# Hybrid Hyena and GLA block: attention operands stored in the layout in which they are loaded, projection columns regrouped, and the sums of the second product's weights set later

## The chip, the cores and the metric

One core of one Trainium2 chip runs the whole block in one launch. The metric is the device time of one launch in microseconds (us). The kernel before has three runs, and one more execution was profiled.

The core's engines each work through an instruction queue of their own: TensorE (PE, matrix products, with its weight loads listed as PEld), VectorE (DVE), ScalarE (ACT), GpSimd (POOL) and SyncE (SP, which here issues nearly all DMA transfers). Semaphores tie them together. An instruction whose input isn't there yet stops everything behind it in its own engine's queue.

## The reference

One layer of a diffusion backbone, in float32, on 2048 tokens of width 1024, with 256 context tokens ahead of them:

```python
h_lat = _rms_norm(x, norm_mix) * (1 + sc1) + sh1
hy, q, k, v, og, gf, gb = split(h_lat @ w_in)        # 1536, 256, 256, 512, 512, 16, 16 columns
# context tokens: the same projection gives only the start states s_f, s_b of the attention
y_gla = (rms(gla_forward + gla_backward) * g_norm) * silu(og)      # 4 heads, chunks of 64 tokens
y_hy  = x0 * (long_conv(x1 * v))                     # FFT convolution over 2048 tokens, 512 channels
x = x + g1 * (concat(y_hy, y_gla) @ w_out)
h2 = _rms_norm(x, norm_mlp) * (1 + sc2) + sh2
x = x + g2 * (square(relu(h2 @ w_mlp1)) @ w_mlp2)    # 1024 -> 4096 -> 1024
out = _rms_norm(x, norm_final)
```

The filter's spectrum for the long convolution is computed in the kernel too.

## The kernel before, in words

Every float32 operand of a product is split into a rounded high part and a low rest, and one product becomes three matmuls (high by high, high by low, low by high). The two MLP products also use a seven-product scheme for 2 by 2 blocks (Strassen's kind), so the blocks of both matrices are added and subtracted before they are multiplied.

The work runs in stages. All times here are microseconds of the profiled execution.

- To about 270: the filter network, its spectrum (`kernel_steps`, `second` stores pieces of it to the DRAM tensor `d_s`), and the context path (`context_steps`).
- 270 to 830: the projections of the 2048 tokens. `token_major(grp, w, tbs)` multiplies blocks of 128 tokens by 264 columns of `w_in`. The 1056 columns of v, og and the two gates make four groups (`grp` 0 to 3) of 264 columns, so a group may hold the end of v and the start of og, or the end of og and the 32 gate columns. v goes by DVE to the DRAM tensor `d_v`, og by Silu on ACT and a multiplication on POOL to `d_og`, and the gates are kept for a transpose.
- 830 to about 1125: the convolution (`conv_steps`, 32 turns: two halves of the channels with 16 turns each), interleaved with the attention (`states`, `weights`, `outputs`). A convolution turn `t` loads four DFT blocks every second turn (tiles `dff`, `dfi`) and the spectrum's real and imaginary pieces (`kr`, `ki`). PE multiplies by `dff` (L945), ACT copies to `sw`, DVE multiplies `kr` (L951, L953), POOL multiplies `sw` by `ki` (L952), and PE goes on with `kr` (L962). The pools hold 2 `dff`, 3 `dfi`, 5 `kr` and 3 `ki`. Attention loads a whole head of v (`vv`, 1 MB), of keys (`kt`, 1 MB) and og in quarters (`og`).
- to about 1960: the output product, then the first MLP product (`ps`, L1384), whose results go through DRAM (`d_m`).
- 1960 to 2679: the second MLP product, 64 turns named `at`, which are 8 passes over 8 blocks of 256 tokens. A turn has 7 products of 6 matmuls each (`full2`, L1640). After each, DVE adds the result into `acc` (`more`, L1645) and the PSUM buffer becomes free for PE. ACT rounds the next turn's left operand (`uh`, L1597), POOL makes its rest (`ul`, L1598).

Every four turns of the second product a new 1 MB piece of `w_mlp2` is loaded to a tile `raw`. Its four quarters are multiplied by the gate `g2` on POOL (`gate`, L1461), and then DVE makes two differences of them, the sums of the change's name:

```python
lambda: dve.tensor_sub(r[:, 4, :], r[:, 3, :], r[:, 0, :]),   # L1464
lambda: dve.tensor_sub(r[:, 3, :], r[:, 2, :], r[:, 3, :])    # L1465
```

`split` (L231, L232) then makes high and low parts of them. `slot()` is called six times in a turn and takes one such step off the list `prep` each time. The code's order is only a wish. The instructions of each engine are arranged when the program is built, by data, buffers and estimated durations, so a step can stand well ahead of the place at which the code calls it.

At the start of the second product `load_u(0)`, `load_u(1)`, `load_acc(0)`, `load_u(2)` and `load_acc(1)` are called in this order. `load_u` fills a tile `ur` with two or three transfers, `load_acc` fetches 1 MB of residual rows.

Of the kernel before, what the change touches and what calls it, by code (L numbers as in the profile page):

```python
# [10 lines left out]
F32 = mybir.dt.float32  # L11
# [7 lines left out]
P = 128  # L19
D = 1024  # L20
T = 2048
# [103 lines left out]
def layout(x):  # L125
# [36 lines left out]
    o["wada1"] = np.stack([blk(wa[:, i * 256:(i + 1) * 256]) for i in range(8)])  # L162
    o["wada2"] = np.stack([blk(wa[:, 2 * D + i * P:2 * D + (i + 1) * P]) for i in range(32)])
    wi = x["w_in"][0]
    o["wi_vg"] = np.stack([blk(wi[:, 2048 + i * 264:2048 + (i + 1) * 264]) for i in range(4)])
    two = lambda a, b: np.concatenate([blk(wi[:, a:a + P]), blk(wi[:, b:b + P])], axis=2)
    o["wi_qk"] = np.stack([two(1536 + i * P, 1792 + i * P) for i in range(2)])
    o["wi_xv"] = np.stack([two(512 + i * P, 1024 + i * P) for i in range(4)])
    o["wi_x0"] = np.stack([blk(wi[:, i * P:(i + 1) * P]) for i in range(4)])
# [41 lines left out]
def hybrid_block(ctx: ExitStack, tc, a, out, dbg=None):  # L211
# [20 lines left out]
        dve.tensor_sub(lo, src, hi.bitcast(F32))  # L232

    dr = ctx.enter_context(tc.tile_pool(name="dram", bufs=1, space=DRAM))
    d_s = dr.tile([32, 128, DH], F32, name="d_s")
    d_s0 = dr.tile([1, DH], F32, name="d_s0")
    d_q = dr.tile([2, 256, T], F32, name="d_q")
    d_ki = dr.tile([2, 256, T], F32, name="d_ki")
    d_kt = dr.tile([NH, P, 16, 2, 64], F32, name="d_kt")
    d_dec = dr.tile([2, 256, 32], F32, name="d_dec")  # L240
    d_v = dr.tile([T, 512], F32, name="d_v")
    d_og = dr.tile([T, 512], F32, name="d_og")
    d_u = dr.tile([DH, T], F32, name="d_u")
    d_x0 = dr.tile([DH, T], F32, name="d_x0")
    d_yt = dr.tile([D, T], F32, name="d_yt")
# [108 lines left out]
    with ExitStack() as ek:  # L354
# [114 lines left out]
        def context_steps():  # L469
# [11 lines left out]
            yield from norm_out(xc, hch, hcl, 1)  # L481
            vc = xp.tile([P, 2, 512], F32, name="vc")
            gc = xp.tile([P, 2, 32], F32, name="gc")
            for g_, c0, n in ((3, 232, 32), (0, 0, 264), (1, 0, 264)):
                hi, lo = load_w(a["wi_vg"][g_][:, :, c0:c0 + n])
                for i in range(2):
                    pp = pt("pc")
                    for k in range(KD):
                        ts = slice(i * P, (i + 1) * P)
                        mm3(pp[:, 0:n], hch[:, k, ts], hcl[:, k, ts], hi[:, k, 0:n], lo[:, k, 0:n],  # L490
                            k == 0, k == KD - 1)
                    if g_ == 0:
                        nc.scalar.copy(vc[:, i, 0:264], pp[:, 0:264])
                    elif g_ == 1:
                        nc.scalar.copy(vc[:, i, 264:512], pp[:, 0:248])
                    else:
                        nc.scalar.copy(gc[:, i, :], pp[:, 0:32])
                    yield W["c_proj"]
# [57 lines left out]
        def kernel_steps():  # L556
            for hc in range(2):
# [73 lines left out]
                def second(t):  # L631
                    zt, dff = st.pop(t)
                    kk = 2 * t
                    pu = pt("pu")
                    for s in range(2):
                        q = (kk + s) % 4
                        mm(pu[:, s * 256:(s + 1) * 256], dff[:, q * P:(q + 1) * P], zt[:, s * 256:(s + 1) * 256],
                           start=True, stop=True)
                    ks = kt_("kb", "ks")
                    nc.scalar.copy(ks[:], pu[:])  # L640
                    k3 = ks[:].rearrange("p (k c) -> p k c", k=2)
                    if t == 0:

                        dma(d_s0[:, cs], k3[127:128, 0, :])
                        dma(d_s[0, 127:128, cs], zrow[0:1, :])
                        dma(d_s[0, 0:127, cs], k3[0:127, 0, :])
                        dma(d_s[1, :, cs], k3[:, 1, :])
                    else:
                        dma(d_s[kk:kk + 2, :, cs].rearrange("k p c -> p k c"), k3)

                yield from staged(16, fetch, turn, second, w=W["k_turn"])

# [16 lines left out]
    rst = ap.tile([P, 512], F32, name="rst")  # L669
    dma(rst[:], a["reset"])  # L670

    def token_major(grp, w, tbs):

        c0 = 264 * grp
        hi, lo = w
        vn = max(0, min(264, 512 - c0))
        on = min(1024 - c0, 264) - vn
        o0 = max(0, c0 - 512)
        for tb in tbs:
            if grp == 3:  # L680
                gs = ap.tile([P, 4, 32], F32, tag="gs", bufs=2, name="gs")
            for i in range(4):
                pp = pt("pv")
                ts = slice(i * P, (i + 1) * P)
                for k in range(KD):
                    mm3(pp[:, 0:264], hts[tb][0][:, k, ts], hts[tb][1][:, k, ts], hi[:, k, :], lo[:, k, :],
                        k == 0, k == KD - 1)
                rows = slice(tb * 512 + i * P, tb * 512 + (i + 1) * P)
                st = ap.tile([P, 512], F32, tag=("gt1", "glg")[i % 2], bufs=2, name="st")
                if vn:  # L690
                    dve.tensor_copy(st[:, 0:vn], pp[:, 0:vn])
                    dma(d_v[rows, c0:c0 + vn], st[:, 0:vn])
                if on:
                    act(st[:, vn:vn + on], pp[:, vn:vn + on], AF.Silu)
                    gps.tensor_mul(st[:, vn:vn + on], st[:, vn:vn + on], gnf[:, o0:o0 + on])
                    dma(d_og[rows, o0:o0 + on], st[:, vn:vn + on])
                if grp == 3:
                    dve.tensor_copy(gs[:, i, :], pp[:, 232:264])
                yield 2.7
            if grp == 3:  # L700
                pg = pt("pg")
                for i in range(4):
                    tr(pg[0:32, i * P:(i + 1) * P], gs[:, i, :], ident)
                dve.tensor_copy(gt[tb * 32:(tb + 1) * 32, :], pg[0:32, :])

    def mod_block(j):
# [116 lines left out]
    def load_kv(h, part=None):  # L823
        if part != 1:
            kt = pre.tile([P, 16, 2, 64], F32, tag="kt", bufs=1, name="kt")
            dma(kt[:], d_kt[h])
            heads[h, "kt"] = kt
        if part != 0:
            vv = gpool(h).tile([P, 16, P], F32, tag="vv", bufs=1, name="vv")
            dma(vv[:], d_v[:, h * P:(h + 1) * P].rearrange("(b p) e -> p b e", p=P))  # L830
            heads[h, "kv"] = (heads[h, "kt"], vv)

    def load_u(ct):
# [48 lines left out]
    def conv_steps():  # L882
        for hc in range(2):
# [29 lines left out]
            def k0(t):  # L913
                kk = 2 * t
                if t % 2 == 0:
                    st["f", t // 2] = ft("dff", 2, "dff")
                    dma(st["f", t // 2][:], a["dft_f"][:, kk:kk + 4, :].rearrange("p k n -> p (k n)"))
                    st["i", t // 2] = ft("dfi", 3, "dfi")
                    dma(st["i", t // 2][:], a["dft_i"][:, kk:kk + 4, :].rearrange("p k n -> p (k n)"))
                kr, ki = ft("kr", 5, "kr"), ft("ki", 3, "ki")  # L920
                for h in range(2):
                    hs = slice(h * 64, (h + 1) * 64)
                    dma(kr[hs].rearrange("p (k c) -> p k c", k=2), d_s[kk:kk + 2, 0:64, cs].rearrange("k p c -> p k c"))
                    dma(ki[hs].rearrange("p (k c) -> p k c", k=2), d_s[kk:kk + 2, 64:128, cs].rearrange("k p c -> p k c"))
                if t == 0:
                    dma(kr[127:128, 0:256], d_s0[:, cs])
                st["k", t] = (kr, ki)
# [181 lines left out]

    def load_og(h, q):  # L1110
        og = gp.tile([P, 4, P], F32, tag="og", bufs=4, name="og")
        dma(og[:], d_og[q * DH:(q + 1) * DH, h * P:(h + 1) * P].rearrange("(b p) e -> p b e", p=P))
        heads[h, "og", q] = og

    def outputs(h, q):
# [274 lines left out]
    def keep(ps, tag):  # L1390
        t = us.tile([P, 512], F32, tag=tag, bufs=2, name=tag)
        nc.scalar.copy(t[:], ps[:])  # L1392
        return t
# [58 lines left out]

    w2s, w2r = {}, {}

    def w2_raw(n, engs):

        r = w2r[n] = raw_tile()
        dma(r[:, 0:4, :], a["w2"][n])

        def gate(q):  # L1460
            engs[q].tensor_mul(r[:, q, :], r[:, q, :], g2b[:, (q // 2) * 512:(q // 2 + 1) * 512])  # L1461

        return [*(lambda q=q: gate(q) for q in range(4)),
                lambda: dve.tensor_sub(r[:, 4, :], r[:, 3, :], r[:, 0, :]),  # L1464
                lambda: dve.tensor_sub(r[:, 3, :], r[:, 2, :], r[:, 3, :])]  # L1465

    def w2_split(n, m):
        r, j, k = w2r[n], PR[m][1], PR[m][0]
# [11 lines left out]
    for tb in range(2):  # L1480
# [8 lines left out]
        for at in range(1, 16):  # L1489
# [33 lines left out]
            if at == 15 and tb == 0:  # L1523
                raws.append(fill_raw(1, 1, gps))
            elif at == 15:
                more_w2 = w2_raw(1, [dve, gps, gps, dve])
                for q in (1, 2):
                    more_w2.pop(1)()
            full(x, w, 6, False)
            u2 = keep(x, "u2")  # L1530
            first(6)
# [5 lines left out]
                nxt[5] = w_split(rn, 5)  # L1537
            full(x, w, 7, False)
            u3 = keep(x, "u3")
            put(n, tb, 1, 1, y, u3)  # L1540
            first(7)
            if rn is not None:
# [56 lines left out]
        ops[at, m] = (hi, lo)  # L1599

    load_u(0)
    load_u(1)
    first_u.update({(h, m): u_tile(0, h, m) for h, m in U0})
    acc4 = {}

# [8 lines left out]
        return acc4[t // 2][:, 2 * (t % 2) + i, j * 512:(j + 1) * 512]  # L1614

    load_acc(0)
    for m in (1, 2, 6):
        w2_split(1, m)
        split_u(0, m)
# [1 line left out]
        w2_split(1, m)  # L1621
    load_u(2)
    load_acc(1)
    held = []
    for f in puts:
        f()
    for step in held:
# [44 lines left out]
    def slot():  # L1672

        for todo in (prep, ends):
            if todo:
                todo.pop(0)()

    sums, prep, ends = {}, [], []
    late = None
# [1 line left out]
    for at in range(NU):  # L1681
# [25 lines left out]
            load_acc(t + 2)  # L1707
        if at + 3 < NU:
            load_u(at + 3)
        if at % 4 == 0:  # L1710
            coming = w2_raw(row(at + 4, 1, 1 - at // 4 % 2), [gps] * 4)
        if at == 40:
            nf = mf.tile([P, D], F32, name="nf")
            dma(nf[:], a["norm_final"].partition_broadcast(P))
# [55 lines left out]
```

## Time and profile before

| | |
|---|---|
| runs | 2690.41, 2690.08, 2682.15 us; median 2690.08 |
| profiled execution | 2681.11 us, span 2679.3 us, mean granted clock 0.963 |
| mean memory traffic | 152 GB/s; 406.09 MB in 304480 packets |
| packets under 2 KB | 226712 |
| HBM read, written | 273.49 MB, 130.09 MB |

The span runs from the first to the last instruction. The granted clock is the share of full speed that TensorE was given. Busy time of an engine is a sum over stages with different limits, so the stages are read one by one. An idle stretch of PE is put down to what released it.

### The profile page before, as it was taken

The page shows a single profiled execution, that of the slowest core. Times are in us where ns is not written, and L with a number is a line of the kernel's source. Part 1 is how long each engine was busy: PE and PEld are TensorE (multiplying, and loading weights), DVE is VectorE, ACT ScalarE, POOL GpSimd, SP SyncE. Part 2 cuts the span into 40 slices and gives each one's busy share as a digit, 9 for nine tenths or more (in the row PEclk, how much of TensorE's full clock was granted, in tenths as well). Part 3 has the DMA queues.
Part 4 walks back from the last instruction along what each step waited for, and adds up shares of the span by engine and source line. Part 5 has one row for each costly group of instructions (what it writes and reads, how often), then busy time and mean ns, then how long its engine had stood idle before and what let it go on. Part 6 is the DMA issues. An engine that isn't in the chain of part 4 may idle for free. (4 is left out here: it accounts for less than half of the span.)

```text
span 2679.3 us, 38019 instructions
## 1 busy us (share of the span) xinstructions
PE 2497.2 (93%) x13320; PEld 2068.7 (77%) x13320; DVE 1613.7 (60%) x2619; ACT 1186.3 (44%) x2273; POOL 1077.1 (40%) x1093
## 2 busy tenths in 40 slices
PE   9799999999998788899989998999978999998997
PEld 5678978898887777788778887888857777777776
DVE  5754366735567677744465557555565656565668
ACT  6464352225225555434555555555543333333334
POOL 2130231214112223132244443544456666666575
PEclk9899999999998798899999999999989999999999
DMA  5425444432547777556444545545474233323233
GB/s 195 147 80 175 124 135 141 139 110 98 175 148 198 202 242 199 198 164 212 154 149 138 165 139 169 170 140 165 135 285 151 99 114 105 119 101 114 99 132 135
DMA packets 304480, 406.09 MB, mean 152 GB/s; under 512 B 25108, under 2 KB 226712, under 8 KB 293920
## 3 DMA queue, kind: packets, MB, share of 16 engines
q1 hardware_dynamic: 301408, 395.27, 46.7%
q10 hardware_dynamic: 2880, 8.39, 0.8%
q8 instruction: 105, 1.72, 0.3%
q14 instruction: 87, 0.71, 0.1%
HBM read 273.49 MB, written 130.09 MB: 151 GB/s over the span
## 5 line engine op out<-in xcount | busy, mean ns | idle before, releaser
L1598 POOL TENSOR_TENSOR ul<-ur,uh 128x256 fp32r<-128x256 f32 x441 | 362.5, 830 | 209.6 <-ACT uh L1597 208.3
L1645 DVE TENSOR_TENSOR acc<-acc,ps 128x512 f32<-128x512 f32 x448 | 303.8, 682 | 153.4 <-PE ps L1640 150.4
L1597 ACT CAST uh<-ur 128x256 fp32r<-128x256 f32 x448 | 179.8, 406 | 408.8 <-PE ps L1640 387.5
L1384 PE MATMUL ps<-bh,wh 128*128 128x512 f32 x896 | 350.4, 393 | 5.8 <-ACT u L1392 3.1
L1384 PE MATMUL ps<-bl,wh 128*128 128x512 f32 x896 | 351.0, 392 | 4.1 <-DVE bl L232 4.1
L1384 PE MATMUL ps<-bh,wl 128*128 128x512 f32 x896 | 350.4, 392 | 4.1 <-DVE wl L232 4.1
L232 DVE TENSOR_TENSOR wl<-raw,wh 128x512 fp32r<-128x512 f32 x276 | 266.7, 978 | 97.0 <-ACT wh L231 94.2
L231 ACT CAST wh<-raw 128x512 fp32r<-128x512 f32 x276 | 170.6, 622 | 201.8 <-PE ps L1384 165.5
L1640 PE MATMUL ps<-wh,uh 128*128 128x512 f32 x448 | 183.5, 410 | 66.4 <-DVE acc L1645 58.2
L1384 PEld LDWEIGHTS ps<-bh,wh 128*128 128x128 f32 x896 | 169.6, 189 | 43.0 <-ACT u L1392 3.7
L1384 PEld LDWEIGHTS ps<-bh,wl 128*128 128x128 f32 x896 | 169.3, 189 | 40.7 <-DVE wl L232 5.3
L1384 PEld LDWEIGHTS ps<-bl,wh 128*128 128x128 f32 x896 | 169.3, 189 | 40.2 <-DVE bl L232 5.3
L1640 PE MATMUL ps<-wh,ul 128*128 128x512 f32 x448 | 179.4, 400 | 0.3 <-DVE ul L1598 0.2
L1640 PE MATMUL ps<-bh,uh 128*128 128x512 f32 x448 | 179.5, 401 | 0.0
L1640 PE MATMUL ps<-bl,uh 128*128 128x512 f32 x448 | 179.5, 401 | 0.0
L1640 PE MATMUL ps<-wl,uh 128*128 128x512 f32 x448 | 179.2, 400 | 0.0
L1640 PE MATMUL ps<-bh,ul 128*128 128x512 f32 x448 | 179.0, 400 | 0.0
L1640 PEld LDWEIGHTS ps<-wh,uh 128*128 128x128 f32 x448 | 87.8, 196 | 96.0 <-DVE acc L1645 63.3
L226 PE MATMUL ph<-hth,whi 128*128 128x512 f32 x384 | 150.9, 393 | 0.0
L226 PE MATMUL pv<-whi,hth 128*128 128x264 f32 x512 | 147.2, 288 | 2.8 <-ACT whi L231 2.6
L228 PE MATMUL ph<-hth,wlo 128*128 128x512 f32 x384 | 149.6, 390 | 0.2 <-DVE wlo L232 0.2
L227 PE MATMUL ph<-htl,whi 128*128 128x512 f32 x384 | 149.4, 389 | 0.0
(289 smaller groups left out, 5713.1 us busy)
## 6 DMA issues: line engine op xcount, KB each, us to landing
raw<-in_w_dram SPq DMA_DIRECT2D x49, 1024.0 KB, 5.5
ur<-d_m SPq DMA_DIRECT2D x112, 448.0 KB, 3.7
d_m<-c SPq DMA_DIRECT2D x128, 256.0 KB, 2.5
d_m<-s SPq DMA_DIRECT2D x96, 256.0 KB, 3.4
xt<-in_x_dram SPq DMA_DIRECT2D x32, 512.0 KB, 5.0
mwt<-in_wada_dram SPq DMA_DIRECT2D x64, 256.0 KB, 3.0
raw<-in_wi_vg_dram SPq DMA_DIRECT2D x20, 528.0 KB, 4.8
wada<-in_wada_dram SPq DMA_DIRECT2D x16, 512.0 KB, 7.6
```

The source lines that it names most:

```text
L226: mm(ps, lh, rh, start=first, stop=False)
L227: mm(ps, lh, rl, start=False, stop=False)
L228: mm(ps, ll, rh, start=False, stop=last)
L231: nc.scalar.copy(hi, src)
L232: dve.tensor_sub(lo, src, hi.bitcast(F32))
L1384: mm(ps[:], x_[:, sl], y_[j], start=start and i == 0, stop=stop and i == 2, skip_group_check=True)
L1597: nc.scalar.copy(hi[:], src)
L1598: (gps if at else dve).tensor_sub(lo[:], src, hi[:].bitcast(F32))
L1640: mm(ps[:], x_[:, kb, :], y_[:], start=start and kb + i == 0, stop=kb == 1 and i == 2, skip_group_check=True)
L1645: dve.tensor_add(acc(t, i, j), acc(t, i, j), ps[:])
```

## The change

Layout, for the attention and the convolution (the mixers):

- The gate columns are dealt out: each of the four groups now has 256 columns of v or og and 8 gate columns, so groups 0 and 1 are v, groups 2 and 3 are og. `token_major` has one store in place of one or two for a block, and every group copies its 8 gate columns to one tile `gs`. The context path loads the 32 gate columns from an array of their own and takes 256 columns of v at a time.
- `d_v` and `d_og` are laid out by head, then by partition. A load of `vv` reads 8 KB in one piece for a partition and one of `og` 2 KB, where both read pieces of 512 bytes before. The stores write two pieces of 512 bytes for a partition in place of one of 1056, 992 or 928 bytes.
- `d_s` holds, for each half of the channels and each turn, 2 KB in one piece for a partition. `kr` and `ki` are loaded with one transfer of 256 KB each, which reads 64 rows twice (a broadcast), in place of two transfers of 128 KB with pieces of 1 KB.

Second product: in the first piece of weights the two sums go to POOL, for the later pieces the code puts empty slots between the gates and ahead of the sums and calls the load one turn earlier, the piece prepared at the end of the first product has all four gates on DVE, and `load_acc(0)` is called ahead of `load_u(1)`.

```diff
-    d_s = dr.tile([32, 128, DH], F32, name="d_s")
+    d_s = dr.tile([2, 16, 128, 2, 256], F32, name="d_s")
-    d_v = dr.tile([T, 512], F32, name="d_v")
-    d_og = dr.tile([T, 512], F32, name="d_og")
+    d_v = dr.tile([NH, P, 16, P], F32, name="d_v")
+    d_og = dr.tile([NH, P, 16, P], F32, name="d_og")
...
-                        dma(d_s[kk:kk + 2, :, cs].rearrange("k p c -> p k c"), k3)
+                        dma(d_s[hc, t], k3)
...
-                if vn:
-                    dve.tensor_copy(st[:, 0:vn], pp[:, 0:vn])
-                    dma(d_v[rows, c0:c0 + vn], st[:, 0:vn])
-                if on:
-                    act(st[:, vn:vn + on], pp[:, vn:vn + on], AF.Silu)
-                    gps.tensor_mul(st[:, vn:vn + on], st[:, vn:vn + on], gnf[:, o0:o0 + on])
-                    dma(d_og[rows, o0:o0 + on], st[:, vn:vn + on])
-                if grp == 3:
-                    dve.tensor_copy(gs[:, i, :], pp[:, 232:264])
+                if grp < 2:
+                    dve.tensor_copy(st[:, 0:256], pp[:, 0:256])
+                else:
+                    act(st[:, 0:256], pp[:, 0:256], AF.Silu)
+                    gps.tensor_mul(st[:, 0:256], st[:, 0:256], gnf[:, (grp - 2) * 256:(grp - 1) * 256])
+                hs = slice(2 * (grp % 2), 2 * (grp % 2) + 2)
+                dma((d_v, d_og)[grp // 2][hs, :, 4 * tb + i, :].rearrange("h p e -> p h e"),
+                    st[:, 0:256].rearrange("p (h e) -> p h e", h=2))
+                dve.tensor_copy(gs[:, tb, i, 8 * grp:8 * grp + 8], pp[:, 256:264])
...
-            dma(vv[:], d_v[:, h * P:(h + 1) * P].rearrange("(b p) e -> p b e", p=P))
+            dma(vv[:], d_v[h])
...
-                for h in range(2):
-                    hs = slice(h * 64, (h + 1) * 64)
-                    dma(kr[hs].rearrange("p (k c) -> p k c", k=2), d_s[kk:kk + 2, 0:64, cs].rearrange("k p c -> p k c"))
-                    dma(ki[hs].rearrange("p (k c) -> p k c", k=2), d_s[kk:kk + 2, 64:128, cs].rearrange("k p c -> p k c"))
+                for v, hs in ((kr, slice(0, 64)), (ki, slice(64, 128))):
+                    dma(v[:], d_s[hc, t, hs].rearrange("p k c -> p (k c)").partition_broadcast(2))
...
-        dma(og[:], d_og[q * DH:(q + 1) * DH, h * P:(h + 1) * P].rearrange("(b p) e -> p b e", p=P))
+        dma(og[:], d_og[h, :, 4 * q:4 * q + 4, :])
...
-                more_w2 = w2_raw(1, [dve, gps, gps, dve])
-                for q in (1, 2):
-                    more_w2.pop(1)()
+                more_w2 = w2_raw(1, [dve] * 4)
...
     load_u(0)
-    load_u(1)
...
     load_acc(0)
+    load_u(1)
...
-        if at % 4 == 0:
-            coming = w2_raw(row(at + 4, 1, 1 - at // 4 % 2), [gps] * 4)
+        if at == 0:
+            coming = w2_raw(row(4, 1, 1), [gps] * 4, gps)
+        elif at % 4 == 3 and at < 60:
+
+            q = w2_raw(row(at + 5, 1, at // 4 % 2), [gps] * 4)
+            coming = [v for step in q[:4] for v in (None, step)] + [None] * 3 + [q[4], None, q[5]]
```

What the program's order becomes is seen at three places. The first is DVE in the second product (turn 13), where the sums of a new piece stand between the additions into `acc`. Before (L1645 are the additions, L1464 and L1465 the sums, L232 the low parts):

```order
L1645 TENSOR_TENSOR acc<-acc,ps 128x512 x7
L1464 TENSOR_TENSOR raw<-raw 128x512
L1645 TENSOR_TENSOR acc<-acc,ps 128x512
L1465 TENSOR_TENSOR raw<-raw 128x512
L1645 TENSOR_TENSOR acc<-acc,ps 128x512
L232 TENSOR_TENSOR wl<-raw,wh 128x512
```

And now (L1638 are the additions, L1457 and L1458 the sums, L234 the low parts):

```order
L1638 TENSOR_TENSOR acc<-acc,ps 128x512 x7
L1457 TENSOR_TENSOR raw<-raw 128x512
L1638 TENSOR_TENSOR acc<-acc,ps 128x512
L1458 TENSOR_TENSOR raw<-raw 128x512
L1638 TENSOR_TENSOR acc<-acc,ps 128x512
L234 TENSOR_TENSOR wl<-raw,wh 128x512
```

Nothing moved here but the line numbers; from turn 5 to the end all five engines have the same order as before.

The second place is POOL at the start of the second product. Before (L1598 is `ul`, L1461 the gates):

```order
L1598 TENSOR_TENSOR ul<-ur,uh 128x256 x12
L1461 TENSOR_TENSOR raw<-raw,g2b 128x512 x4
L1598 TENSOR_TENSOR ul<-ur,uh 128x256 x21
L1461 TENSOR_TENSOR raw<-raw,g2b 128x512 x3
L1598 TENSOR_TENSOR ul<-ur,uh 128x256
```

And now (L1592 is `ul`, L1454 the gates, L1457 and L1458 the sums):

```order
L1592 TENSOR_TENSOR ul<-ur,uh 128x256 x9
L1454 TENSOR_TENSOR raw<-raw,g2b 128x512 x4
L1592 TENSOR_TENSOR ul<-ur,uh 128x256
L1457 TENSOR_TENSOR raw<-raw 128x512
L1592 TENSOR_TENSOR ul<-ur,uh 128x256
L1458 TENSOR_TENSOR raw<-raw 128x512
L1592 TENSOR_TENSOR ul<-ur,uh 128x256 x15
L1454 TENSOR_TENSOR raw<-raw,g2b 128x512 x3
```

The first piece's gates stand three `ul` earlier and its sums are on POOL. The second piece's gates follow after 17 `ul` in place of 21.

The third place is SP in the convolution's first turns, up to the third load of `dff`, the one at 854.03 in the profile. Before:

```order
L1112 DMA og<-d_og 128x4x128 x2
L826 DMA kt<-d_kt 128x2048
L830 DMA vv<-d_v 128x16x128
L924 DMA ki<-d_s 64x2x256 x2
L917 DMA dff<-in_dft_f_dram 128x512
```

And now:

```order
L1105 DMA og<-d_og 128x512 x2
L825 DMA vv<-d_v 128x2048
L821 DMA kt<-d_kt 128x2048
L1105 DMA og<-d_og 128x512
L1048 DMA dc<-d_dec 64x32
L1049 DMA qi<-d_q 64x2048
L917 DMA ki<-d_s 128x1x512
L912 DMA dff<-in_dft_f_dram 128x512
```

A third `og` quarter (256 KB), a small `dc` and half of a head's queries `qi` (512 KB) came ahead of this `dff`. At the start of the second product SP has the first `acc` load behind two `ur` loads, where it was ahead of all six.

More of the change, by code (lines that the diff above doesn't have):

```diff
@@ L164, in layout @@
     wi = x["w_in"][0]
-    o["wi_vg"] = np.stack([blk(wi[:, 2048 + i * 264:2048 + (i + 1) * 264]) for i in range(4)])
-    two = lambda a, b: np.concatenate([blk(wi[:, a:a + P]), blk(wi[:, b:b + P])], axis=2)
+    two = lambda a, b, n=P, m=P: np.concatenate([blk(wi[:, a:a + n]), blk(wi[:, b:b + m])], axis=2)
+    o["wi_vg"] = np.stack([two(2048 + i * 256, 3072 + i * 8, 256, 8) for i in range(4)])
+    o["wi_gk"] = blk(wi[:, 3072:3104])
     o["wi_qk"] = np.stack([two(1536 + i * P, 1792 + i * P) for i in range(2)])
@@ L483, in context_steps @@
             gc = xp.tile([P, 2, 32], F32, name="gc")
-            for g_, c0, n in ((3, 232, 32), (0, 0, 264), (1, 0, 264)):
-                hi, lo = load_w(a["wi_vg"][g_][:, :, c0:c0 + n])
+            for g_, n in ((2, 32), (0, 256), (1, 256)):
+                hi, lo = load_w(a["wi_gk"] if g_ == 2 else a["wi_vg"][g_][:, :, 0:n])
                 for i in range(2):
@@ L491, in context_steps @@
                             k == 0, k == KD - 1)
[L492 to L495, printed above, removed]
+                    if g_ < 2:
+                        nc.scalar.copy(vc[:, i, g_ * 256:(g_ + 1) * 256], pp[:, 0:256])
                     else:
@@ L644, in second @@
                         dma(d_s0[:, cs], k3[127:128, 0, :])
-                        dma(d_s[0, 127:128, cs], zrow[0:1, :])
-                        dma(d_s[0, 0:127, cs], k3[0:127, 0, :])
-                        dma(d_s[1, :, cs], k3[:, 1, :])
+                        dma(d_s[hc, 0, 127:128, 0], zrow[0:1, :])
+                        dma(d_s[hc, 0, 0:127, 0], k3[0:127, 0, :])
+                        dma(d_s[hc, 0, :, 1], k3[:, 1, :])
                     else:
-                        dma(d_s[kk:kk + 2, :, cs].rearrange("k p c -> p k c"), k3)
+                        dma(d_s[hc, t], k3)
                 yield from staged(16, fetch, turn, second, w=W["k_turn"])
@@ L670, in hybrid_block @@
     dma(rst[:], a["reset"])
+    gs = ap.tile([P, 4, 4, 32], F32, name="gs")
     def token_major(grp, w, tbs):
-        c0 = 264 * grp
         hi, lo = w
-        vn = max(0, min(264, 512 - c0))
-        on = min(1024 - c0, 264) - vn
-        o0 = max(0, c0 - 512)
         for tb in tbs:
-            if grp == 3:
-                gs = ap.tile([P, 4, 32], F32, tag="gs", bufs=2, name="gs")
             for i in range(4):
@@ L687, in token_major @@
                         k == 0, k == KD - 1)
-                rows = slice(tb * 512 + i * P, tb * 512 + (i + 1) * P)
                 st = ap.tile([P, 512], F32, tag=("gt1", "glg")[i % 2], bufs=2, name="st")
-                if vn:
-                    dve.tensor_copy(st[:, 0:vn], pp[:, 0:vn])
-                    dma(d_v[rows, c0:c0 + vn], st[:, 0:vn])
-                if on:
-                    act(st[:, vn:vn + on], pp[:, vn:vn + on], AF.Silu)
-                    gps.tensor_mul(st[:, vn:vn + on], st[:, vn:vn + on], gnf[:, o0:o0 + on])
-                    dma(d_og[rows, o0:o0 + on], st[:, vn:vn + on])
-                if grp == 3:
-                    dve.tensor_copy(gs[:, i, :], pp[:, 232:264])
+                if grp < 2:
[7 more added lines that the diff above has]
+                dve.tensor_copy(gs[:, tb, i, 8 * grp:8 * grp + 8], pp[:, 256:264])
                 yield 2.7
@@ L702, in token_major @@
                 for i in range(4):
-                    tr(pg[0:32, i * P:(i + 1) * P], gs[:, i, :], ident)
+                    tr(pg[0:32, i * P:(i + 1) * P], gs[:, tb, i, :], ident)
                 dve.tensor_copy(gt[tb * 32:(tb + 1) * 32, :], pg[0:32, :])
@@ L1453, in hybrid_block, with w2_raw @@
     w2s, w2r = {}, {}
-    def w2_raw(n, engs):
+    def w2_raw(n, engs, eng=dve):
         r = w2r[n] = raw_tile()
@@ L1463, in w2_raw @@
         return [*(lambda q=q: gate(q) for q in range(4)),
-                lambda: dve.tensor_sub(r[:, 4, :], r[:, 3, :], r[:, 0, :]),
-                lambda: dve.tensor_sub(r[:, 3, :], r[:, 2, :], r[:, 3, :])]
+                lambda: eng.tensor_sub(r[:, 4, :], r[:, 3, :], r[:, 0, :]),
+                lambda: eng.tensor_sub(r[:, 3, :], r[:, 2, :], r[:, 3, :])]
     def w2_split(n, m):
@@ L1539, in hybrid_block @@
             u3 = keep(x, "u3")
+            if tb and at == 15:
+                held = []
             put(n, tb, 1, 1, y, u3)
@@ L1623, in hybrid_block @@
     load_acc(1)
-    held = []
     for f in puts:
@@ L1674, in slot @@
         for todo in (prep, ends):
-            if todo:
-                todo.pop(0)()
+            step = todo.pop(0) if todo else None
+            if step:
+                step()
     sums, prep, ends = {}, [], []
```

## The prediction

> **What bounds the kernel now.** I read the page first: busy time by engine, the DMA queues, and of the groups ACT's casts (busy us, mean ns), and of the DMA issues the row of `ur` (count, KB each, us to landing).
>
> ```profile
> span 2679.3 us, 38019 instructions
> PE 2497.2 (93%) x13320; PEld 2068.7 (77%) x13320; DVE 1613.7 (60%) x2619; ACT 1186.3 (44%) x2273; POOL 1077.1 (40%) x1093
> q1 hardware_dynamic: 301408, 395.27, 46.7%
> q10 hardware_dynamic: 2880, 8.39, 0.8%
> L231 ACT CAST wh<-raw 128x512 fp32r<-128x512 f32 x276 | 170.6, 622 | 201.8 <-PE ps L1384 165.5
> ur<-d_m SPq DMA_DIRECT2D x112, 448.0 KB, 3.7
> ```
>
> PE is the bound, 93% busy. A change that takes no matmul away can win only its 182 us of idle time and the time it runs at a lower clock. So the next view is the busy time by stage: the stretch, then PE, PEld, DVE, ACT and POOL busy, the granted clock, the DMA engines' share and GB/s.
>
> ```profile
> 270.00:830.00 560.00, 554.27 (x3095) 476.44 (x3094) 315.19 (x594) 186.98 (x316) 130.49 (x138) 0.99 0.43 135
> 830.00:860.00 30.00, 21.25 (x180) 17.56 (x179) 26.94 (x60) 16.67 (x30) 4.62 (x4) 0.88 0.94 236
> 860.00:900.00 40.00, 32.01 (x290) 28.48 (x292) 26.47 (x52) 22.11 (x42) 16.12 (x16) 0.80 0.74 200
> 900.00:930.00 30.00, 22.87 (x145) 20.74 (x144) 21.00 (x50) 15.79 (x30) 4.57 (x4) 0.73 0.89 262
> 930.00:990.00 60.00, 54.91 (x591) 48.42 (x590) 42.71 (x97) 29.31 (x52) 8.25 (x12) 0.99 0.80 241
> 830.00:1125.00 295.00, 246.25 (x2355) 214.69 (x2355) 219.38 (x464) 153.17 (x279) 73.00 (x76) 0.88 0.72 208
> 1960.00:1990.00 30.00, 18.52 (x66) 13.81 (x66) 15.76 (x24) 10.82 (x30) 22.10 (x23) 0.82 1.03 392
> 1990.00:2580.00 590.00, 543.85 (x2289) 443.67 (x2290) 362.35 (x536) 205.70 (x477) 381.33 (x441) 0.96 0.34 118
> ```
>
> The projections (270 to 830) have nothing to give: PE idles 5.7 us. The convolution (830 to 1125) loses 48.8 us, with the DMA engines near full at first. The second product loses 46 us in 590, with DMA at a third. The waits say on what. From the whole trace, PE's and DVE's largest:
>
> ```profile
> PE ps L1640 <- DVE acc L1645: 58.2, 25, 4.5
> PE pu L945 <- DMA dff<-in_dft_f_dram: 16.0, 3, 7.5
> PE ps L1640 <- ACT uh L1597: 8.0, 2, 7.6
> PE p L962 <- DVE kr L953: 7.0, 2, 5.7
> PE pd L1074 <- DMA vv<-d_v: 2.8, 1, 2.8
> DVE raw L1464 <- POOL raw L1461: 83.5, 17, 6.2
> ```
>
> The chain of waits shows how the first row comes about. Start, length, what; from the first piece of weights and a later one:
>
> ```profile
> 1986.16 1.12 POOL raw L1461
> 1987.31 1.20 DVE raw L1464
> 1988.51 0.60 DVE acc L1645
> 1990.45 28.75 PE ps L1640 x113
> ...
> 2043.53 38.65 PE ps L1640 x162
> 2083.55 1.23 POOL raw L1461
> 2084.81 1.20 DVE raw L1464
> 2086.01 0.60 DVE acc L1645
> 2087.86 4.38 PE ps L1640 x11
> ```
>
> The sum L1464 stands in DVE's queue ahead of additions whose results are ready. It waits for POOL's last gate, the additions wait behind it, PSUM fills up, and PE stops. PE ends at 2082.18 (2043.53 + 38.65) and resumes at 2087.86.
>
> PE's own rows around the start of the second product give two more numbers (start, length, matmul, idle before it and what ended it); below them, SP's rows.
>
> ```profile
> 1953.53 0.50 PE L1384 MATMUL ps<-bh,wh 128*128 128x512 f32 x1 [3.08 <-ACT u L1392]
> 1966.93 0.79 PE L1640 MATMUL ps<-wh,uh 128*128 128x512 f32 x1 [7.62 <-ACT uh L1597]
> 1970.26 0.63 PE L1640 MATMUL ps<-wh,uh 128*128 128x512 f32 x1
> 1972.39 0.49 PE L1640 MATMUL ps<-bh,ul 128*128 128x512 f32 x1
> 1978.03 0.39 PE L1640 MATMUL ps<-wl,uh 128*128 128x512 f32 x1
> 1983.47 0.39 PE L1640 MATMUL ps<-wl,uh 128*128 128x512 f32 x1
> ...
> 1958.33 0.58 SPq L1611 DMA_DIRECT2D acc<-d_x  x1
> 1958.96 3.58 SPq L1582 DMA_DIRECT2D ur<-d_m  x6
> ```
>
> From 1978.03 to 1983.47 PE starts 24 matmuls, one in 0.227 us. From 1970.26 to 1972.39, behind the idle 7.62 us, it starts five, one in 0.426 us. So a stop costs its idle time and a slow restart. For the stops of the second product that is measured in the chain: 162 matmuls took 38.65 us, and at 0.227 they take 36.8, so the restart costs 1.9 us.
>
> **The change, part by part.**
>
> Second product, later pieces: nothing. The code sets the sums later, but in the order of the program they stand behind the last gate and among the same additions as before (turn 13 is shown above, and all turns from 5 on agree). The piece moved from turn 4 to turn 3 keeps its sums on DVE behind four gates on POOL, so its stop moves and stays. The 64 turns load sixteen pieces, so fifteen stops remain.
>
> Second product, first piece: its sums leave DVE, so nothing stands ahead of the additions there. The stop from 1986.13 (POOL row at 1986.16) to 1990.45, 4.3 us, goes with its restart of 1.9: 6.2 us. What is late next: POOL does two sums more, 2 × 1.2 us by its own gates (1.23) and by DVE's sum (1.20), and the `ul` behind them come 2.4 us later. POOL is busy 381 of 590 us and stands ahead of PE here (9 `ul` before the gates, a turn needs 7), so this is hidden. If it is not, 2.4 us come back with a restart of 1.9. I take 6.2, with ends 8 and 2.
>
> Start of the second product: PE waits 7.62 us for `uh`, which waits for `ur`. SP issues `acc` (1 MB) first and the six `ur` behind it. The DMA engines are full, at 392 GB/s, so 1.05 MB takes 2.7 us, and the issue 0.6. Now two `ur` go first. Ends: 0, if the transfers already share the engines evenly, and 3.3. I take 2.7: a share of 1.03 leaves no room for both, and the usual landing of `ur`, 3.7 us, shows how much of the 7.62 is the rest.
>
> The page "TensorE: Matmul & The Clock Gate" of the Trainium skill (Part 1: The HAM clock gate) says that the clock halves behind about 3.4 us of idleness and comes back after about as long at work. The 0.426 against 0.227 us behind 7.62 us of idleness agree. By that rule 4.9 us of idleness are still punished, and this term gets no clock gain; without it up to 2 us more could come.
>
> End of the first product: two gates of the prepared piece go from POOL to DVE, and a cast on ACT stands behind the copy for which PE waits 3.08 us. The cast is 0.62 us; I take 0.6, ends 0 and 1.5.
>
> Projections and context: 64 small copies of 8 columns on DVE in place of 16 of 32, and 16 Silu and 16 products on POOL of 16 columns fall away. Even at a whole addition's 0.60 us, 48 more copies are 29 us on a DVE that is idle for 245 of these 560 us. The stores have twice the pieces at a DMA share of 0.43, and nothing in this stage waits for them. The 96 context matmuls are 8 of 264 columns shorter: 8/512 × 0.227 × 96 = 0.3 us. Ends: +3 (PSUM is held until the copy is done) and −1. I take −0.3.
>
> Convolution. A price of a packet first. q1: 46.7% of 16 × 2679.3 us over 301408 packets of 1311 bytes is 66 ns; q10: 0.8% over 2880 packets of 2913 bytes is 119 ns. Through both points a packet costs about 23 ns and 0.033 ns a byte, an estimate: 40 ns for 512 bytes, 57 for 1 KB, 90 for 2 KB, 292 for 8 KB. `kr` and `ki`: 16384 packets of 1 KB become 8192 of 2 KB, 934 us become 737, over 16 engines 12 us less. `vv` in this stage: three of four, 6144 packets of 512 bytes become 384 of 8 KB, 8 us less. `og`: 8192 become 2048 of 2 KB, 9 us less. That is 29 us off the 0.72 × 295 = 212 us of DMA time.
>
> How much of it does PE see? It waits for loads directly for 16.0 + 2.8 us, and for 7.0 through `kr`, which stands behind POOL and a load. With a restart of 1.9 us behind three of the stops (the clock is 0.80 and 0.73 here, where 0.99 is usual) at most 31 us could go. Three things hold against all of it. DVE is busy 26.94 of the first 30 us and takes over as the bound there. SP's order puts 768 KB of `og` and `qi` ahead of the third `dff`, for which PE waits: 3.3 us at 236 GB/s, which eats half of that wait's gain. And late waits, 990 on, come where DMA is less full. I take 10 us, a third of the bound, with ends 31 and −4 (the 3.3 us added at one wait, with nothing saved).
>
> Sum: 6.2 + 2.7 + 0.6 + 0.3 + 10 = 19.8, so 2681.1 − 19.8 = 2661 for an execution like the profiled one (the span 2679.3 and 1.8 around it). The median of the runs is 9 above the profile, two runs there and one beside it. I put the changed kernel's median halfway, at 2666.
>
> **The rivals.**
>
> The sums do move on the chip as the code says, and fifteen more stops go: 58.2 − 4.3 = 54 us of waits and 15 × 1.9 of restarts, 82 us, to 2584. Against it: the order. Chance 0.04.
>
> The convolution gains nothing, since bytes bound it: 2676. For it: the same bytes move and the loads compete with each other. Against it: the DMA share is 0.94 at 236 GB/s there, and 1.03 at 392 where pieces are larger, so pieces cost. Chance 0.24. The page "DMA: Bandwidth & Descriptors" of the Trainium skill (Specifications) names 512 bytes as the least transfer for line rate, by which all pieces here moved at full rate before; the 236 GB/s at 0.94 speak against that rule.
>
> The convolution gains nearly all, 30 us: 2646. Against it: DVE at 26.94 of 30. Chance 0.08.
>
> Slower: a `kr` or `ki` tile now comes by one transfer that reads rows twice. If it lands 1 us later in each of 32 turns and only three `ki` tiles are at hand, POOL's product and then PE wait: 32 us in place of the gain of 10, so 2666 + 42 = 2708. It decides against the kernel from 0.6 us a turn on, where all 19.8 are gone. Against it: half the packets, half the issues on SP. Chance 0.08.
>
> **How the numbers follow.** The forecast has 0.56: 2666, by itself 2650 to 2682. From 2638 (most of the large gain) to 2690 (a loss of the whole gain) the case of no gain is in, and half of each of the two ends is out: 8 in 10 or a little more. About 0.3%, 8 us, is what can be told from no change, so faster is below 2682. Faster: 0.51 of the forecast's 0.56, 0.11 of the 0.24, 0.08 and 0.04, 0.74. Same: the rest of those two, less 0.01, 0.17. Slower: 0.08 and that 0.01, 0.09.
>
> **What would show it.** Right: PE's wait for `acc` falls from 58.2 to about 54, with stops every four turns from turn 3 on; the 7.62 falls to about 5; the waits for `dff` and `vv` fall by about half, and DMA's share in 830 to 900 falls at more GB/s per share. Wrong: stops of second-product turns that vanish or come at `ul`, or a wait for `ki` in the convolution that grows.

## The result, and the profile after

The changed kernel takes 2935.81 us (median of four runs, 2924.23 to 2941.1) where the kernel before takes 2687.86 (median of four). The ratio is 1.093, 95% interval 1.090 to 1.095: 9% slower, where 1% faster was forecast. The profiled execution took 2924.23 us, 243 us more than the one before.

The page of the changed kernel shows that PE did the same work and waited more (2497.2 us busy before, now 2521.4 at a lower clock, in a span that is 242.9 longer):

```profile
span 2922.2 us, 37847 instructions
PE 2521.4 (86%) x13320; PEld 2088.8 (71%) x13320; DVE 1614.5 (55%) x2667; ACT 1183.3 (40%) x2257; POOL 1073.7 (37%) x1077
q1 hardware_dynamic: 280288, 395.19, 42.5%
```

The same bytes went in fewer packets and in less DMA time in sum. By stage (the columns are those of the table in the prediction):

```profile
270.00:830.00 560.00, 554.55 (x3110) 477.13 (x3108) 319.18 (x629) 186.21 (x304) 124.58 (x126) 1.00 0.43 135
830.00:860.00 30.00, 18.34 (x165) 15.38 (x163) 21.44 (x49) 14.32 (x26) 2.52 (x2) 0.83 0.24 78
860.00:900.00 40.00, 5.27 (x31) 4.60 (x28) 7.82 (x14) 3.03 (x6) 3.75 (x3) 0.57 0.45 130
930.00:990.00 60.00, 17.30 (x116) 15.15 (x116) 12.20 (x25) 12.07 (x23) 7.83 (x9) 0.61 0.30 88
1125.00:1320.00 195.00, 92.18 (x698) 79.14 (x699) 71.88 (x154) 57.62 (x109) 28.73 (x28) 0.72 0.28 91
```

The projections are untouched. The convolution collapses: PE works 5 of 40 us at 860, and the DMA engines, 94% busy in the stretch from 830 before, are now 24% to 45% busy in these stretches while PE and POOL wait for loads. A wait for memory at a low DMA share is the sign to read here: it isn't bandwidth that lacks, the engines are not all at work. The waits of PE over the whole trace, then POOL's for `ki` (total us, times, longest us), now and, in the last line, before:

```profile
PE pu L938 <- DMA dff<-in_dft_f_dram: 172.6, 11, 34.7
PE ps L1633 <- DVE acc L1638: 59.9, 25, 5.7
PE p L955 <- DVE kr L946: 36.5, 4, 11.8
PE ps L1633 <- ACT uh L1591: 7.6, 2, 6.0
...
POOL sw L945 <- DMA ki<-d_s: 271.3, 26, 28.4
POOL sw L952 <- DMA ki<-d_s: 22.1, 5, 8.0
```

A wait for `ki` that grows is one of the signs of being wrong that the prediction named.

SP's own rows (start, length, what), and a window of 5 us inside the `ki` issue at 919.99 (columns as in the table by stage), show why:

```profile
899.07 5.20 SPq L1048 DMA_DIRECT2D dc<-d_dec  x1
...
914.65 5.24 SPq L917 DMA_DIRECT2D kr<-d_s  x1
919.99 5.17 SPq L917 DMA_DIRECT2D ki<-d_s  x1
925.26 5.14 SPq L912 DMA_DIRECT2D dff<-in_dft_f_dram  x1
930.45 0.49 SPq L1051 DMA_DIRECT2D ki<-d_ki  x1
...
920.00:925.00 5.00, 5.00 (x45) 4.28 (x44) 1.11 (x2) 1.96 (x4) 0.00 (x0) 0.67 0.13 49
```

49 GB/s at a share of 0.13: that is two of sixteen DMA engines at work. 256 KB then take 5.2 us, and SP, which issued a load of `ki` in 0.6 us before, now gets one out every 5.3 us or so, with `dff` in the queue behind. The held issue need not be the slow transfer's own: the one of `dff` takes 5.14 us, and that of `dc`, which is 8 KB, 5.20 (0.57 in the median before). So the length of an issue tells how fast the queue in front of it drains.

In the second product the 15 later stops are there, as forecast. The start is not as forecast. The chain of waits (start, length, what; small rows left out):

```profile
2230.01 3.79 POOL raw L1454 x3
2233.80 0.71 POOL ul L1592
2234.52 0.32 SPq L1576
2234.88 4.18 DMA ur<-d_m
2239.44 0.63 ACT bh L233
2242.22 1.13 DVE bl L234
2245.30 9.77 PE ps L1633 x30
2256.65 1.18 POOL raw L1454
2260.99 0.67 DVE acc L1638
2263.52 24.24 PE ps L1633 x96
2288.34 1.21 DVE raw L1457
2291.40 8.72 PE ps L1633 x30
```

Stops of PE end at 2245.30 (3.53 us idle), 2263.52 (5.74) and 2291.40 (2.30). The first has a new cause: ACT's cast `bh` stands behind casts that wait for a late `ur`, DVE's `bl` waits for it, and the additions stand behind `bl`. The `ur` is late because SP issues it only behind a `ul` of POOL, and that `ul` stands behind the four gates of the first piece. The second stop is that of the piece moved forward, and the third is the first of those that come every four turns.

### The profile page after: what moved, and what is told of

It reads as the page before. It is cut to its first block, busy times and chain, and to the rows that moved or that the text cites. A ratio compares the mean times of both kernels' runs of the same rounds, so it can differ in the third digit from the quotient of the medians.

```text
span 2922.2 us, 37847 instructions
## 1 busy us (share of the span) xinstructions
PE 2521.4 (86%) x13320; PEld 2088.8 (71%) x13320; DVE 1614.5 (55%) x2667; ACT 1183.3 (40%) x2257; POOL 1073.7 (37%) x1077
## 5 line engine op out<-in xcount | busy, mean ns | idle before, releaser
L1592 POOL TENSOR_TENSOR ul<-ur,uh 128x256 fp32r<-128x256 f32 x441 | 364.9, 836 | 194.5 <-ACT uh L1591 194.1
L1638 DVE TENSOR_TENSOR acc<-acc,ps 128x512 f32<-128x512 f32 x448 | 303.6, 682 | 147.8 <-PE ps L1633 145.2
L234 DVE TENSOR_TENSOR wl<-raw,wh 128x512 fp32r<-128x512 f32 x276 | 268.0, 983 | 96.8 <-ACT wh L233 94.2
L1633 PE MATMUL ps<-wh,uh 128*128 128x512 f32 x448 | 182.5, 407 | 67.6 <-DVE acc L1638 59.9
L938 PE MATMUL pu<-zt,dff 128*128 128x256 f32 x128 | 47.8, 511 | 190.4 <-DMA dff<-in_dft_f_dram 172.6
L938 PEld LDWEIGHTS pu<-zt,dff 128*128 128x128 f32 x128 | 29.8, 258 | 197.4 <-issue 192.4
L945 POOL TENSOR_TENSOR sw<-sw,ki 128x512 f32<-128x512 f32 x32 | 40.6, 1270 | 348.1 <-DMA ki<-d_s 271.3
```

Of the source, the lines that this page charges most:

```text
L945: gps.tensor_mul(sw[:], sw[:], ki[:])
L1592: (gps if at else dve).tensor_sub(lo[:], src, hi[:].bitcast(F32))
L1633: mm(ps[:], x_[:, kb, :], y_[:], start=start and kb + i == 0, stop=kb == 1 and i == 2, skip_group_check=True)
L1638: dve.tensor_add(acc(t, i, j), acc(t, i, j), ps[:])
```

## The experiments

Ratios are to the kernel before on the same chip, with 95% intervals.

**Two plain transfers.** The changed kernel with one edit:

```diff
-                for v, hs in ((kr, slice(0, 64)), (ki, slice(64, 128))):
-                    dma(v[:], d_s[hc, t, hs].rearrange("p k c -> p (k c)").partition_broadcast(2))
+                for h in range(2):
+                    for v, hs in ((kr, slice(0, 64)), (ki, slice(64, 128))):
+                        dma(v[h * 64:(h + 1) * 64], d_s[hc, t, hs].rearrange("p k c -> p (k c)"))
```

> The changed kernel, but each kr and ki tile comes by two plain transfers of 64 partitions with 2 KB a row, in place of one transfer that reads 64 rows twice. Theory: the whole loss lies in that broadcast transfer, which the trace shows at about 49 GB/s with a tenth of the DMA engines busy, 5.2 us for 256 KB. Then the time falls to the forecast without it, 2660 to 2685 us, and PE's wait for dff falls from 172.6 us to under 16. Rival: the loss comes from the new order on SP (og, dc and qi ahead of dff) or from stores of 512-byte pieces; then it stays above 2850 us.

Measured: 2675.32 us, ratio 0.997 (0.996 to 0.999). The theory held, the rival fell. Its SP rows and its waits:

```profile
L918 SPq DMA_DIRECT2D ki<-d_s x64: 444/551/1351, 825.1 to 1045.5; - x64
...
PE ps L1634 <- DVE acc L1639: 57.7, 24, 5.5
PE pu L939 <- DMA dff<-in_dft_f_dram: 13.1, 4, 5.2
```

An issue takes 0.55 us in the median (the middle of the three numbers, in ns), and the wait for `dff` is back at 13.1 us.

**The broadcast alone.** The kernel before with the new `d_s` and the broadcast line.

> The kernel before with the new layout of d_s and the broadcast transfers for kr and ki alone; v, og, gates and the second product as before. Theory: all of the loss is here, 2900 to 2960 us. Rival (order on SP, layouts of v and og): no more than 2750 us.

Measured: 2936.09 us, ratio 1.095 (1.091 to 1.099), PE's wait for `dff` 187.2 us. All of the loss is in this part.

**The new layout of `d_s` with plain transfers.** It differs from the last kernel in the one line shown above.

> The kernel before with the new layout of d_s alone, kr and ki by two plain transfers each with 2 KB a row in place of two pieces of 1 KB. It differs from the kernel with the broadcast alone in that one line. Theory: 2675 to 2692 us, since 12 us less DMA time, by the estimate of a packet's price, is at most half seen by PE. Rival: pieces of 1 KB cost nothing, 2688 us.

Measured: 2682.54 us, ratio 1.000 (0.998 to 1.003). So the line costs about 254 us, and pieces of 2 KB in place of 1 KB bring nothing that can be told.

**The second product alone.** The kernel before with that part of the change.

> The kernel before with the second product's part of the change alone. Theory: the later pieces keep their stops, and the first piece's stop is replaced by one at a late load of ur and by a longer one at the piece moved forward, as the trace of the changed kernel has them (waits over 1 us from the second product on: 65.0 us against 64.3); 2680 to 2692 us, no change. Rival, the forecast: 9.5 us less, about 2678 us. Rival, the sums really move: 2600 us.

Measured: 2680.54 us, ratio 0.999 (0.998 to 1.001): no change. The forecast's 9.5 us would be a ratio of 0.996, outside the interval.

**How many engines.** The changed kernel, reading 32 rows four times, or 8 rows sixteen times, with the same bytes and pieces written to the tiles. The other rows are left out, so these two don't compute the layer's result:

```diff
-                    dma(v[:], d_s[hc, t, hs].rearrange("p k c -> p (k c)").partition_broadcast(2))
+                    dma(v[:], d_s[hc, t, hs.start:hs.start + 32].rearrange("p k c -> p (k c)").partition_broadcast(4))
```

> The changed kernel, but each kr and ki transfer reads 32 rows four times in place of 64 rows twice: the same 256 KB, 128 pieces of 2 KB and the same place on SP; rows 32 to 63 of each are left out, so the convolution is computed with the wrong spectrum. Theory: the transfer's outermost dimension sets how many of the 16 DMA engines work on it, four in place of two, so 2.6 us each in place of 5.2; the 64 transfers take 168 us of a stage of 295 us and mostly hide: 2680 to 2750 us. Rival: reading a row again is slow in itself, then it stays at 2930 us or above.

> As the kernel that reads 32 rows four times, but 8 rows sixteen times; the other rows are left out. Theory: all 16 engines share each transfer, 0.7 us for 256 KB, and the time is that of plain transfers or a little less, 2660 to 2680 us. Rival (reading again is slow): 2930 us or more.

Measured: 2776.14 us with four (ratio 1.034, 1.030 to 1.037), 2666.9 with sixteen (0.993, 0.991 to 0.995). SP's rows for `ki` of the changed kernel, of four and of sixteen:

```profile
L917 SPq DMA_DIRECT2D ki<-d_s x32: 513/5172/7942, 825.4 to 1283.5; - x32
```

```profile
L917 SPq DMA_DIRECT2D ki<-d_s x32: 505/2168/5597, 823.8 to 1124.5; - x32
```

```profile
L917 SPq DMA_DIRECT2D ki<-d_s x32: 514/521/1051, 827.1 to 1036.2; - x32
```

The issue falls from 5.17 to 2.17 and 0.52 us. A window with four copies, within the held issue that follows a `ki`, has twice the share and twice the rate of the one above, as four engines in place of two would:

```profile
887.50:890.00 2.50, 1.93 (x5) 1.60 (x6) 0.00 (x1) 0.00 (x0) 0.00 (x0) 0.50 0.26 97
```

So reading rows again costs nothing that shows with sixteen copies, and what costs is a small number of copies, which is the transfer's outermost dimension. Sixteen come out a little below the plain transfers (0.993 against 0.997), but they read only 8 different rows, so the complete load might not. That four would mostly hide was a miss: the range ended at 2750 us. Its waits for `dff` still add up to 59.0 us; why so much is left wasn't tried.

**v and og alone.** The kernel before with regrouped columns and the new layout of `d_v` and `d_og`.

> The kernel before with the projection's columns regrouped and v and og in the new layout; d_s, kr, ki and the second product as before. Theory: of the 8 us that the changed kernel gains with plain transfers, neither the second product nor d_s alone shows any, so it is here: 2672 to 2680 us, where the kernel before has 2683 to 2685. Rival: the parts only count together, then no change, 2680 us or more.

Measured: 2676.09 us, ratio 0.998 (0.996 to 0.999). It is as large as the whole gain with plain transfers (0.997), so that gain is here as far as can be told. The traces narrow it to a stage. PE's rows for the products with `dff` in the convolution (shortest, median and longest in ns, first and last start), in the kernel before and in this one:

```profile
L945 PE MATMUL pu<-zt,dff x128: 379/379/792, 842.9 to 1048.1; 128*128 128x256 f32 x128
L940 PE MATMUL pu<-zt,dff x128: 379/379/795, 842.7 to 1042.2; 128*128 128x256 f32 x128
```

This stretch starts at the same time and ends 6 us earlier, of 8.2 us between the two profiles. So the projections, with their 16 small products fewer, gave nothing here, and the loads of the convolution and the attention are the likely place. It is one profile each: with the layout of `d_s` alone, where no gain is shown, the same stretch is 2.6 us shorter than before.

**The sums of all pieces on POOL.** On top of two plain transfers:

```diff
-            q = w2_raw(row(at + 5, 1, at // 4 % 2), [gps] * 4)
+            q = w2_raw(row(at + 5, 1, at // 4 % 2), [gps] * 4, gps)
```

> The changed kernel with two plain transfers for each kr and ki tile, and in the second product the two sums of every piece on POOL, not of the first alone. Theory: each stop comes from a sum that stands on DVE ahead of ready additions and waits for POOL's last gate, so the stops of the fourteen or fifteen later pieces go, idle time and slow restart together about 5 us each: 70 us less than with two plain transfers alone, 2600 to 2620 us. Rival: POOL, with two sums of 1.3 us more behind four gates, makes the rests ul late and PE waits for them instead; then 2650 us or more.

Measured: 2619.3 us, ratio 0.976 (0.974 to 0.977). The wait for `acc` falls from 57.7 us with plain transfers to 26.6:

```profile
PE ps L1634 <- DVE acc L1639: 26.6, 18, 9.4
```

The theory of the stops held: 56 us less for 15 pieces (58 by the ratios, as the two kernels ran on different chips), 3.7 us each, at the weak end of what was expected. The longest stop, 9.4 us in the third turn, is not at a sum of a later piece: there DVE's `bl` waits 5.15 us for ACT's `bh`, as in the chain above, and then takes 6.00 us, which stays unexplained.

**The gates of the later pieces on DVE**, `[dve] * 4` in that line and the sums on DVE too.

> The changed kernel with two plain transfers for each kr and ki tile, and in the second product the gates of the later pieces on DVE with the sums, so that no sum waits for POOL. Theory: the wait for POOL goes; the four gates (about 0.65 us each) and the sums stand between additions that have slack, and PE stops for less than 2 us at a piece: 2600 to 2640 us. Rival: DVE gets 2.6 us more work per piece and its additions are late by themselves, 2660 us or more.

Measured: 2608.24 us, ratio 0.971 (0.969 to 0.973). DVE does four gates more for a piece, and PE waits less. No gate or sum of a later piece waits for POOL now; the largest stop left, 6.1 us in the third turn, is again behind `bh` (last line; in brackets the idle time before the instruction and what ended it):

```profile
PE pu L939 <- DMA dff<-in_dft_f_dram: 16.2, 4, 6.4
PE ps L1634 <- DVE acc L1639: 14.3, 11, 6.1
...
1988.31 1.33 DVE L234 TENSOR_TENSOR bl<-raw,bh 128x512 fp32r<-128x512 f32 x1 [6.54 <-ACT bh L233]
```

**The same at the old turns.**

```diff
-        if at == 0:
-            coming = w2_raw(row(4, 1, 1), [gps] * 4, gps)
-        elif at % 4 == 3 and at < 60:
...
+        if at % 4 == 0:
+            coming = w2_raw(row(at + 4, 1, 1 - at // 4 % 2), [dve] * 4)
```

> The changed kernel with two plain transfers for each kr and ki tile; in the second product the pieces are called at the turns of the kernel before (every fourth, from 0), with no empty slots, and all gates and sums are on DVE. Theory: the stop of about 6 us at turn 3, which is left with gates on DVE from the second piece on, comes from the piece moved forward and the sums of the first piece on POOL; it goes, so 2595 to 2606 us, a few us under the 2608 with gates on DVE. Rival: that stop comes from the late ur load alone and stays, 2606 us or more.

Measured: 2602.77 us, ratio 0.969 (0.965 to 0.973). It can't be told from the last kernel (0.969 to 0.973). The stop of 6.1 us went, as the theory had it: with the first piece off POOL, and the pieces at the old turns, the stop behind `bh` is gone. But one of 4.7 us came in the second turn, and no time that can be told was won. DVE's row there shows the new cause, the first piece's load, which its gates now wait for ahead of the additions:

```profile
1977.34 1.57 DVE L1455 TENSOR_TENSOR raw<-raw,g2b 128x512 f32<-128x512 f32 x2 [4.39 <-DMA raw<-in_w_dram]
...
PE ps L1634 <- DVE acc L1639: 13.6, 12, 4.7
```

The last two kernels beat both the kernel before and the changed one, by 3% and 11%.

## Why the prediction was wrong

The step that failed is the cost of the one-transfer load of `kr` and `ki`. The prediction priced it by its bytes and pieces ("934 us become 737, over 16 engines 12 us less"), as if every transfer were spread over all sixteen engines. This one runs on two: the share is 0.13 with two copies and 0.26 with four. Its rival "Slower" had the right place, the tiles `kr` and `ki`, and a price that was far too small: 1 us a turn was assumed, where 243 us over 32 turns are 7.6. Its path, over POOL's product to PE, is there (PE's wait for `kr` went from 7.0 to 36.5 us), but PE's larger wait runs over SP's held queue, for `dff` (16.0 to 172.6). How much of the 243 us each would cost without the other wasn't tried. It was given 0.08, because half the packets and half the issues were read as less work. The measurement of an issue in the trace of before (0.6 us on SP for 64 rows of a plain transfer) said nothing of a form that the trace did not contain, and the bound from above for that form was missing: one engine alone. With the prediction's own 90 ns for a packet of 2 KB, one engine's 128 packets make 11.5 us, two engines' 64 make 5.8; 64 transfers at 5.8 are 371 us, more than the whole stage of 295.

The rule was written down. The Trainium skill, "DMA: Bandwidth & Descriptors" (Rules for kernel authors), says that a leading broadcast of c copies confines a transfer to at most c engines. The runs agree: a share of 0.13 for two copies and 0.26 for four, and 5.17, 2.17 and 0.52 us of issue for two, four and sixteen. By it the forecast would have come out the other way.

The other terms, now without that load, where 0.99 was forecast and 0.997 measured:

- Convolution, 10 us forecast. The layout of `d_s` gave nothing (1.000), v and og 0.25%, about 7 us. So the size is about right, with some luck: the part that was put on `kr` and `ki`, 12 of 29 us of DMA time, brought nothing, and the waits that were to fall by half did not. In the four profiles with plain transfers in the changed kernel PE waits 13.1 to 16.2 us for `dff` (16.0 before) and 1.6 to 3.3 for `vv` (2.8). The stretch from 830 to 860 in two of them, with two plain transfers alone and with the gates on DVE as well, which changes nothing in this stage:

```profile
830.00:860.00 30.00, 21.24 (x180) 17.85 (x179) 28.07 (x59) 16.43 (x30) 5.09 (x5) 0.89 0.84 241
830.00:860.00 30.00, 20.07 (x180) 16.78 (x179) 28.04 (x60) 16.35 (x30) 5.53 (x5) 0.97 0.94 248
```

  The DMA share is lower than the 0.94 of before in one and the same in the other, so a fall isn't shown, and PE is busy no longer than before (21.25). DVE is at 28 of 30 us, which fits the reservation that it bounds this stretch; that it does wasn't tested.
- Later pieces of the second product, 0 forecast: right. The waits for `acc` are 59.9 us after, 58.2 before, and the code's empty slots moved nothing.
- First piece, 6.2 us forecast: wrong. Its stop went, and another took its place, from a late `ur` through ACT's cast. The prediction looked at POOL for "what is late next", counted the `ul` behind the two sums and called their delay hidden. The chain runs through the `ul` ahead of the sums, right behind the four gates, and through what waits for that `ul`: SP's issue of the next `ur`. By itself the second product's part gives 0.999.
- Start of the second product, 2.7 us forecast: the step was misread. The first `acc` load still stands ahead of the first `ur`; what moved is the second load of `acc`, and it moved forward, from behind six `ur` to behind two. The text above the prediction says otherwise and is wrong there. SP's rows; the first line is the second `acc` load before, the others are the changed kernel's:

```profile
1962.59 0.44 SPq L1611 DMA_DIRECT2D acc<-d_x  x1
...
2205.19 0.38 SPq L1604 DMA_DIRECT2D acc<-d_x  x1
2205.62 0.97 SPq L1576 DMA_DIRECT2D ur<-d_m  x2
2206.69 0.69 SPq L1604 DMA_DIRECT2D acc<-d_x  x1
2207.47 2.26 SPq L1576 DMA_DIRECT2D ur<-d_m  x4
```

  The longest wait for `uh` is 6.0 us now, where it was 7.6. Over all profiles it is 5.7 to 7.6 us in the four kernels with the old order and 5.4 to 6.7 in the eight with the new one. About 1 us may be won there; the kernel with the second product's part alone shows none in its time.
- End of the first product, 0.6 us forecast: too small a term for these runs to tell.

The slow restart behind a stop fits too: with the sums on POOL the time fell by 56 us and the waits for `acc` by 31 (57.7 to 26.6); 15 restarts of 1.9 us would make 28.5 us more, 59.6 in all. The granted clock (the third column from the end) says the same of the second product, with two plain transfers and with the sums on POOL as well:

```profile
1960.00:2600.00 640.00, 585.28 (x2446) 476.61 (x2447) 390.49 (x572) 224.20 (x531) 424.60 (x489) 0.95 0.37 130
1960.00:2600.00 640.00, 612.45 (x2656) 499.76 (x2655) 442.14 (x611) 250.14 (x602) 495.20 (x574) 0.99 0.40 138
```

0.04 of 640 us are about 26 us.

## What to carry to other kernels

A transfer's cost is not its bytes and pieces alone: look at its outermost dimension (two, four and sixteen copies made 2936, 2776 and 2667 us here), and when a load is rewritten, bound the new form by the fewest engines that it can run on before counting what fewer packets save. If waits for memory grow while the DMA share falls, look for a transfer on few engines, and for a queue that stands still behind it. And a step that the code sets later has moved only if the program's order shows it; what took the stops away was to remove the wait of one engine for another that stood ahead of urgent work.

## What the runs showed of the hardware that was not expected

Two sixteenths of the DMA engines moved 49 GB/s, some 24 GB/s for each, so 256 KB in pieces of 2 KB took 5.2 us, 81 ns for a piece on its engine; the estimate was 90. The issuing queue was held for the same time (5.17 us in the median), so plain transfers behind it, `dff` above all, were late too.

The clock falls behind shorter stops than the 3.4 us of idleness that the prediction reckoned with. In the trace of before PE stood still for 2.54 us until 2215.35 and for 2.26 us until 2130.13; the granted clock (0.51 and 1.00) was halved behind the first and not behind the second:

```profile
2215.00:2218.40 3.40, 3.05 (x7) 2.47 (x8) 3.38 (x7) 0.41 (x1) 2.69 (x3) 0.51 0.57 229
2130.00:2133.40 3.40, 3.27 (x14) 2.69 (x15) 3.40 (x7) 1.27 (x3) 3.40 (x4) 1.00 0.48 195
```
